# Four token tiles together in the first FFN, and modulation sums queued behind row scaling

## The chip, the cores and the metric

The kernel runs on one core of one Trainium2 chip. The metric is the device time of one execution in microseconds (us). A core has five engines that work side by side, each through its own list of instructions in order: TensorE (PE, matrix products; its weight loads are listed as PEld), VectorE (DVE), ScalarE (ACT), GpSimd (POOL) and SyncE (SP, which here only issues transfers, DMAs, from the chip's memory). Matrix products write to PSUM, and VectorE and ScalarE read from there.

## The reference

The network has two layers over 256 latent tokens and 256 context tokens of 1024 channels, in fp32. Cut to what matters here, it computes:

```python
def modulate(h, g_pre, shift, scale):
    return rms_norm(h, g_pre) * (1 + scale) + shift

def modulation(cond, w, b):            # nine rows of 1024 per condition
    m = jax.nn.silu(cond) @ w + b
    ...

def half_ffn_update(h, mod, k, g_pre, g_post, w_in, w_out):
    y = swiglu(modulate(h, g_pre, mod[3 * k], mod[3 * k + 1]), w_in, w_out)
    return h + FFN_RES_WEIGHT * mod[3 * k + 2] * rms_norm(y, g_post)

for i in range(DEPTH):
    mx = modulation(c, w_mod[i], b_mod[i])
    mc = modulation(c_ctx[None], w_mod[i], b_mod[i])
    x = half_ffn_update(x, mx, 0, ...)        # and the same for the context with mc
    ...                                       # layer 0: recurrent mixer, layer 1: attention
    x = half_ffn_update(x, mx, 2, ...)
```

`swiglu` multiplies by `w_in` (1024 x 5632, a gate half and an up half), forms silu(gate) * up, and multiplies by `w_out` (2816 x 1024).

## The kernel before

**Tiles and precision.** The 512 tokens are four tiles of 128: 0 and 1 are context (`CTX`), 2 and 3 latent (`LAT`), worked in the order 2, 3, 0, 1 (`TILES`). Each fp32 operand is split in two fp32r parts: ScalarE casts the high part (`whi`, `hh`, `dh`, line 114), VectorE subtracts it from the source for the low part (`wlo`, `hl`, `dl`, line 115). A product is three matmuls: high by high, high by low, low by high (lines 151 to 153 in `punit`). A weight tile is loaded by `wslot` into one of five slots (`raw`), 512 KB each; the same five slots take the modulation rows of the background jobs.

**FFN.** `ffn` goes through 22 column blocks of 128 hidden units. For one block `punit` runs a gate unit and an up unit (u = 0, 1) over eight channel blocks k, and `glu` (lines 408 to 414) forms the product and splits it. In a normal FFN the first four columns (`NSPLIT`) run for the latent tokens and then for the context tokens, 256 wide, because the context tiles come later out of the stage before; all other columns run for all 512 tokens. After each group of columns `w_out` is applied.

**The opening.** The very first FFN has no stage before it. `ffn_start` takes its place for the first four columns: in two channel halves (hb) it computes the shift and scale rows by matmuls (`mods_start`, line 295), turns them to columns, applies them to the turned latent rows (`first_pre`, lines 271 to 273), and runs the four columns for the latent tokens. Then `load_ctx` loads, scales and turns the context tiles, and `ffn` runs the four columns for them. `first_scale` and `first_turn` scale the rows and turn them by TensorE (line 201).

**Between stages.** When a stage has the result of a tile, `post` scales it and adds it to the residual stream, and `pre` computes the next row scaling: a mean of squares on ScalarE (line 172), eight VectorE instructions on one value per row (`rstd`, lines 181 to 188), and the scaling (line 194). `pre_turn` follows some units later, turns the tile on TensorE (line 201) and applies shift and scale on ScalarE (line 239).

**Background jobs.** The other modulation rows are computed by VectorE. `mod_job` loads eight pieces of `w_mod` and adds each, times a value of the condition, to a sum (line 365, 1024 wide), for one or both conditions; then a TensorE matmul with ones adds over partitions (line 371), a ScalarE copy (line 392) takes the row out of PSUM and TensorE turns it into columns (line 280), or the row is multiplied by a gain and spilled (lines 378 to 388). `bg(n)` runs n steps of the jobs at marked points of an FFN.

**Order of the work.** No order is written out by hand. The program lists the instructions; when the kernel is built a planner goes through them with a model of their costs, takes among those whose inputs it thinks are there the one listed first (those under `high_priority` ahead), and so fixes one order for each engine and the DMA queue. On the chip each engine follows that order and waits where an input is late. `order(ins)` gives what is listed under it an edge: it comes behind `ins` on that engine.

Of the kernel before, what the change touches and what calls it, by code (L numbers as in the profile page):

```python
# [11 lines left out]
ALU = mybir.AluOpType  # L12
# [24 lines left out]
class Net:  # L37
    def __init__(self, ctx, tc):
# [4 lines left out]
        self.pending = []  # L43
        e = ctx.enter_context
# [209 lines left out]
    def first_scale(self, t):  # L254
        return self.scaled(t, self.m4().rearrange("p a b -> p (a b)"))
# [8 lines left out]
    def first_pre(self, cond, A, S, ks=range(NK)):  # L264
        nc = self.nc
        s = (CTX, LAT)[cond]
# [57 lines left out]
    def ffn_start(self, w_in, w_mod, between):  # L324
        v = w_in.rearrange("(k p) c -> p k c", p=P)
        self.A00 = self.c([P, NK, 2], F32, "A00")
        banks = [self.mm().rearrange("p (u t) -> p u t", u=2) for _ in range(NSPLIT)]
        ws = [[] for _ in range(NSPLIT)]
        for hb in range(2):
            first = self.mods_start(w_mod, hb, between)  # L330
            self.first_pre(1, *first, range(4 * hb, 4 * hb + 4))
            for p in range(NSPLIT // 2):
                for u in range(2):
                    ws[2 * p + u].append(
                        self.wslot([v[:, 4 * hb : 4 * hb + 4, u * DFF + p * 256 : u * DFF + p * 256 + 256]])
                    )
                for o in range(2):
                    for u in range(2):
                        w = [ws[2 * p + u][hb]] * 2
                        self.punit(  # L340
                            banks[2 * p + o][:, u],
                            w,
                            o,
                            LAT,
                            range(4 * hb, 4 * hb + 4),
                            hb == 0 and u == 0,
                            hb == 1,
                        )
                    if hb == 1:
                        self.glu(banks[2 * p + o][:, 0], banks[2 * p + o][:, 1], 2 * p + o, LAT)  # L350
        return ws, first

    def mod_job(self, l, m, conds=(0, 1), f=None):
# [7 lines left out]
        for k in range(NK):  # L361
            raw = self.raw()
            nc.sync.dma_start(raw, self.w_mod[l, k * P : (k + 1) * P, m * D : (m + 1) * D])
            for c in conds:
                v.scalar_tensor_tensor(acc[c], raw, self.cs[:, k, c : c + 1], acc[c], op0=ALU.mult, op1=ALU.add)  # L365
            yield
        ps = self.st()
# [10 lines left out]
        if f is not None:  # L378
            gq = self.s2()
            gi = 3 + m // 3  # L380
            for j in range(4):
                cc = slice((j // 2) * 512, (j // 2) * 512 + 512)
                nc.gpsimd.dma_start(gq[32 * j : 32 * j + 32], self.norm_g[l, gi : gi + 1, cc].to_broadcast((32, 512)))
            row = self.a2()
# [713 lines left out]
```

## Time and profile before

| What | us |
|---|---|
| median of three runs | 1713.89 |
| the three runs | 1711.07, 1713.89, 1714.55 |
| the profiled execution, its own time | 1710.77 |
| its span in the trace | 1709.0 |

The page gives busy times of each engine, the chain of work that ended last, and the costliest groups of instructions. A line of the timeline reads: start, duration, engine, line of the kernel, operation, output tile from input tiles, shapes, how many were merged, and in brackets how long the engine stood idle before it and what ended that. Matmuls overlap, so the distance between two starts tells their rate and not the duration. A line of the windows reads: stretch, its length, busy time of PE, PEld, DVE, ACT and POOL with counts, the granted clock of TensorE as a share of 2.4 GHz, the busy share of the DMA engines, and GB/s.

### The profile page before, as it was taken

The numbers are of one execution on the slowest core, as the hardware profiler recorded it, in microseconds if no ns is written. First come the engines' busy times: TensorE is split into PE (matmuls) and PEld (weight loads), VectorE is DVE, ScalarE is ACT, GpSimd is POOL, SyncE is SP. The second block draws the span as 40 slices with busy tenths as digits, with TensorE's granted clock in tenths as the row PEclk, the third lists the DMA queues.
The fourth block names the chain that finished last, engine by engine and source line by source line (L and its number), as shares of the span: only waits on it lengthen the run. The fifth ranks groups of instructions, "written<-read, shape, count | busy, mean of one in ns | idle before, by whom it ended". The sixth has DMA issues, their size and how long they took to land.

```text
span 1709.0 us, 22391 instructions
## 1 busy us (share of the span) xinstructions
PE 1658.0 (97%) x8744; PEld 1385.9 (81%) x8744; DVE 1118.7 (65%) x1705; ACT 704.7 (41%) x1117; POOL 44.2 (3%) x89
## 2 busy tenths in 40 slices
PE   6999999999999989999999999999999999999997
PEld 4978888888988788888888888878888886679997
DVE  4878677658978785877833695655433687575454
ACT  3423322236699442332222442332232466574442
POOL 0010000000000001000000001000000000000000
PEclk9999999999999999999999999999999999999999
DMA  9366655443233154666433055865332061046561
GB/s 341 132 207 214 202 174 177 147 162 99 79 95 99 50 198 133 211 205 198 156 116 98 26 197 164 293 197 172 108 109 96 29 218 50 1 152 210 169 202 45
DMA packets 163961, 253.39 MB, mean 148 GB/s; under 512 B 9600, under 2 KB 114664, under 8 KB 163856
## 3 DMA queue, kind: packets, MB, share of 16 engines
q1 hardware_dynamic: 159424, 244.35, 43.8%
q0 software_dynamic: 3680, 7.10, 1.4%
q8 instruction: 68, 1.11, 0.3%
q10 hardware_dynamic: 752, 0.53, 0.1%
q14 instruction: 37, 0.30, 0.1%
HBM read 250.84 MB, written 1.10 MB: 147 GB/s over the span
## 4 chain that ended last, share of the span: by engine, by line
PE 77%; DVE 10%; ACT 5%; DMA 5%; issue 2%; ACTq 0%; DVEq 0%
PE mm L151 15%; PE mm L153 15%; PE mm L152 15%; PE mm L166 7%; PE mm L168 7%; PE mm L167 7%; DVE m L365 3%; DMA raw<-in_w_mod_dram 2%; DVE wlo L115 2%; PE mm L877 1%; DMA raw<-in_ffn_w_out_dram 1%; DMA raw<-in_ffn_w_in_dram 1%; ACT whi L114 1%; PE st L914 1%; PE st L903 1%
## 5 line engine op out<-in xcount | busy, mean ns | idle before, releaser
L151 PE MATMUL mm<-hh,whi 128*128 128x512 f32 (+1 forms) x1808 | 615.8, 342 | 8.3 <-ACT hh L271 4.7
L152 PE MATMUL mm<-hl,whi 128*128 128x512 f32 (+1 forms) x1808 | 615.7, 341 | 1.4 <-DVE hl L115 1.0
L153 PE MATMUL mm<-hh,wlo 128*128 128x512 f32 (+1 forms) x1808 | 616.3, 341 | 0.3 <-DVE wlo L115 0.3
L115 DVE TENSOR_TENSOR wlo<-raw,whi 128x1024 fp32r<-128x1024 f32 x316 | 382.4, 1221 | 157.0 <-ACT whi L114 155.3
L114 ACT CAST whi<-raw 128x1024 fp32r<-128x1024 f32 x316 | 330.2, 1053 | 353.4 <-DMA raw<-in_ffn_w_in_dram 107.5
L151 PEld LDWEIGHTS mm<-hh,whi 128*128 128x128 f32 x1808 | 346.0, 192 | 54.4 <-ACT hh L271 5.4
L152 PEld LDWEIGHTS mm<-hl,whi 128*128 128x128 f32 x1808 | 346.5, 192 | 39.5 <-DVE hl L115 1.4
L153 PEld LDWEIGHTS mm<-hh,wlo 128*128 128x128 f32 x1808 | 346.8, 192 | 38.1 <-DVE wlo L115 0.6
L365 DVE SCALAR_TENSOR_TENSOR m<-raw,cs,m 128x1024 f32<-128x1024 f32 x224 | 277.0, 1278 | 47.1 <-DMA raw<-in_w_mod_dram 39.2
L166 PE MATMUL mm<-whi,dh 128*128 128x512 f32 x592 | 232.7, 393 | 4.7 <-ACT dh L114 2.4
L168 PE MATMUL mm<-whi,dl 128*128 128x512 f32 x592 | 231.2, 391 | 0.0
L167 PE MATMUL mm<-wlo,dh 128*128 128x512 f32 x592 | 231.0, 390 | 0.0
L413 DVE TENSOR_TENSOR a<-s,mm 128x512 f32<-128x512 f32 (+1 forms) x96 | 54.5, 568 | 171.0 <-PE mm L153 111.8
L166 PEld LDWEIGHTS mm<-whi,dh 128*128 128x128 f32 x592 | 111.6, 188 | 34.0 <-issue 3.4
L412 ACT ACTIVATE s<-mm 128x512 f32<-128x512 f32 (+1 forms) x96 | 48.3, 503 | 214.1 <-PE mm L153 214.1
L168 PEld LDWEIGHTS mm<-whi,dl 128*128 128x128 f32 x592 | 111.6, 188 | 23.9 <-DVE dl L115 0.4
L167 PEld LDWEIGHTS mm<-wlo,dh 128*128 128x128 f32 x592 | 111.5, 188 | 22.4
L114 ACT CAST dh<-a 128x512 fp32r<-128x512 f32 (+1 forms) x96 | 50.5, 526 | 187.6 <-DVE a L413 187.6
L115 DVE TENSOR_TENSOR dl<-a,dh 128x512 fp32r<-128x512 f32 (+1 forms) x96 | 54.6, 569 | 26.5 <-ACT dh L114 26.3
L239 ACT ACTIVATE tmp<-st,modT,A 128x128 f32<-128x128 f32 x144 | 54.6, 468 | 9.3 <-PE st L201 9.3
L482 DVE TENSOR_TENSOR y<-y,mm 128x512 f32<-128x512 f32 x24 | 16.5, 686 | 38.1 <-PE mm L168 38.1
L172 ACT ACTIVATE tmp<-y 128x1024 f32<-128x1024 f32 x12 | 12.7, 1058 | 58.5 <-DVE y L434 58.5
(212 smaller groups left out, 1311.6 us busy)
## 6 DMA issues: line engine op xcount, KB each, us to landing
raw<-in_ffn_w_in_dram SPq DMA_DIRECT2D x176, 512.0 KB, 4.8
raw<-in_w_mod_dram SPq DMA_DIRECT2D x128, 512.0 KB, 4.4
raw<-in_ffn_w_out_dram SPq DMA_DIRECT2D x88, 512.0 KB, 4.8
wm<-in_w_mod_dram SPq DMA_DIRECT2D x16, 512.0 KB, 7.2
raw<-in_rg_w_in_dram SPq DMA_DIRECT2D x16, 512.0 KB, 3.3
raw<-in_attn_w_qkv_dram SPq DMA_DIRECT2D x12, 512.0 KB, 3.7
g<-spill POOLq DMA_DIRECT2D x16, 256.0 KB, 4.4
raw<-in_rg_gate_w_dram SPq DMA_DIRECT2D x16, 256.0 KB, 3.2
```

What stands on the lines that cost most here:

```text
L114: self.nc.scalar.copy(hi, src)
L115: self.nc.vector.tensor_tensor(lo, src, hi.bitcast(F32), op=ALU.subtract)
L151: nc.tensor.matmul(out, a, xh, start=first and k == ks[0], stop=False, skip_group_check=True)
L152: nc.tensor.matmul(out, a, xl, start=False, stop=False, skip_group_check=True)
L153: nc.tensor.matmul(out, b, xh, start=False, stop=last and k == ks[-1], skip_group_check=True)
L166: nc.tensor.matmul(out, a, wh, start=(k == 0), stop=False)
L167: nc.tensor.matmul(out, a, wl, start=False, stop=False)
L168: nc.tensor.matmul(out, b, wh, start=False, stop=(k == nk - 1))
L239: nc.scalar.activation(hf[:, k * P : (k + 1) * P], ps[:, q * P : (q + 1) * P], AF.Identity, bias=S[:, k, cond : cond + 1], scale=A[:, k, c ...
L365: v.scalar_tensor_tensor(acc[c], raw, self.cs[:, k, c : c + 1], acc[c], op0=ALU.mult, op1=ALU.add)
L412: nc.scalar.activation(a, pg, AF.Silu)
L413: nc.vector.tensor_tensor(b, a, pu, op=ALU.mult)
```

## The change

Three things are changed. First, in the opening all four token tiles are loaded, scaled and turned before the first modulation half is applied; only the first two columns run there, for all 512 tokens and in two channel halves; columns 2 and 3 join the ordinary ones. The turned tiles are copied out of PSUM by ScalarE instead of VectorE. Second, the sums of the background jobs get an edge to the last row scaling that `pre` listed (`chain`), and the end of each job (`mod_sum`, `mod_cols`) is listed at the next background step instead of right behind the sums. Third, a small silu activation is listed at the end of the recurrent mixer.

```diff
     def scaled(self, t, xs):
-        self.nc.vector.tensor_scalar(xs, self.x[:, t], r, RS, op0=ALU.mult, op1=ALU.mult)
+        self.last = self.nc.vector.tensor_scalar(xs, self.x[:, t], r, RS, op0=ALU.mult, op1=ALU.mult)
...
     def pre(self, t, A, S, buf):
         with self.tc.high_priority():
             xs = self.scaled(t, buf)
+        self.chain = self.last
...
     def first_turn(self, t, xs):
         for b in range(2):
             ps = self.turn(xs, b)
-            self.nc.vector.tensor_copy(
+            self.nc.scalar.copy(
...
         for k in ks:
-            a, b = A[:, k, cond : cond + 1], S[:, k, cond : cond + 1]
-            tmp = self.tmp()[:, :HT]
-            nc.scalar.activation(self.hh[:, k, s], yt[:, k, s], AF.Identity, bias=b, scale=a)
-            nc.vector.tensor_scalar(tmp, yt[:, k, s], a, b, op0=ALU.mult, op1=ALU.add)
-            nc.vector.tensor_tensor(self.hl[:, k, s], tmp, self.hh[:, k, s].bitcast(F32), op=ALU.subtract)
+            tmp = self.tmp()[:, :T]
+            for cond, s in ((1, LAT), (0, CTX)):
+                a, b = A[:, k, cond : cond + 1], S[:, k, cond : cond + 1]
+                nc.scalar.activation(self.hh[:, k, s], yt[:, k, s], AF.Identity, bias=b, scale=a)
+                nc.vector.tensor_scalar(tmp[:, s], yt[:, k, s], a, b, op0=ALU.mult, op1=ALU.add)
+            nc.vector.tensor_tensor(self.hl[:, k], tmp, self.hh[:, k].bitcast(F32), op=ALU.subtract)
...
     def ffn_start(self, w_in, w_mod, between):
+        banks = [[self.mm() for u in range(2)] for o in range(2)]
         for hb in range(2):
+            ks = range(4 * hb, 4 * hb + 4)
             first = self.mods_start(w_mod, hb, between)
+            self.first_pre(*first, ks)
+            ws = [[self.wslot([v[:, 4 * hb : 4 * hb + 4, u * DFF : u * DFF + 256]])] * 2 for u in range(2)]
+            for o in range(2):
                 for u in range(2):
+                    self.punit(banks[o][u], ws[u], o, ALL, ks, hb == 0, hb == 1)
+        for o in range(2):
+            self.glu(*banks[o], o, ALL)
...
             for c in conds:
-                v.scalar_tensor_tensor(acc[c], raw, self.cs[:, k, c : c + 1], acc[c], op0=ALU.mult, op1=ALU.add)
+                with self.order(self.chain):
+                    v.scalar_tensor_tensor(acc[c], raw, self.cs[:, k, c : c + 1], acc[c], op0=ALU.mult, op1=ALU.add)
+            if k == NK - 1:
+                self.later.append(lambda: self.mod_sum(l, m, acc, f))
             yield
...
+    def finish_later(self):
+        todo, self.later = self.later, []
+        for f in todo:
+            f()
...
     def load_ctx():
-        between = [norm_cols] + [lambda t=t: N.first_turn(t, xs[t]) for t in TILES[:2]]
-        ws, first = N.ffn_start(ffn_w_in[0, 0], w_mod, between)
-        for t in TILES[2:]:
-            nc.sync.dma_start(N.x[:, t], cx[0, t * P : (t + 1) * P, :])
-            N.first_turn(t, N.first_scale(t))
-        N.first_pre(0, *first)
+        between = [lambda t=t: N.first_turn(t, xs[t]) for t in TILES]
+        between[0] = lambda: (norm_cols(), N.first_turn(TILES[0], xs[TILES[0]]))
+        N.ffn_start(ffn_w_in[0, 0], w_mod, between)
         rg_cols()
...
         def step(n):
+            N.finish_later()
             while n > 0:
...
+    with N.order(prev):
+        sc.activation(N.small([P, 1]), c1[:, 0:1], AF.Silu)
```

`mod_sum` holds the matmul with ones and either the gain and spill or the copy on ScalarE; it lists `mod_cols`, the turn into columns, for the step after. At the end of an FFN whatever is left of both is listed before the rows are loaded.

## Rows read from the trace of the kernel before

**Rows 1.** The page's first part: busy time, share of the span and number of instructions of each engine.

```profile
PE 1658.0 (97%) x8744; PEld 1385.9 (81%) x8744; DVE 1118.7 (65%) x1705; ACT 704.7 (41%) x1117; POOL 44.2 (3%) x89
```

**Rows 2.** Busy times in four stretches: the opening, the first four columns of the second FFN, those of the third, and a place in the third FFN.

```profile
0.00:84.70 84.70, 68.50 (x492) 58.11 (x493) 55.12 (x139) 32.21 (x54) 4.36 (x12) 0.94 0.68 238
602.20:659.70 57.50, 51.18 (x401) 50.33 (x400) 44.11 (x69) 25.00 (x49) 0.00 (x0) 0.94 0.51 168
985.20:1040.40 55.20, 50.95 (x401) 49.91 (x400) 45.72 (x71) 24.49 (x48) 0.00 (x0) 0.94 0.56 184
...
1143.20:1149.20 6.00, 3.41 (x12) 2.76 (x12) 4.43 (x7) 1.10 (x2) 0.03 (x1) 0.72 0.89 301
```

**Rows 3.** The waits of PE over the whole span: what waited for what, total us, times, longest.

```profile
PE st L201 <- DVE y L194: 5.7, 4, 2.5
```

**Rows 4.** The timeline of PE at the start of the second FFN.

```profile
608.08 0.28 PE L152 MATMUL mm<-hl,whi 128*128 128x256 f32 x1
608.20 0.28 PE L153 MATMUL mm<-hh,wlo 128*128 128x256 f32 x1
610.09 1.09 PE L201 MATMUL st<-ident,y 128*128 128x128 f32 x8 [1.62 <-DVE small L183]
...
629.77 1.09 PE L201 MATMUL st<-ident,y 128*128 128x128 f32 x8 [1.68 <-DVE y L194]
632.88 0.74 PE L151 MATMUL mm<-hh,whi 128*128 128x256 f32 x4 [2.02 <-ACT hh L114]
...
640.33 0.29 PE L151 MATMUL mm<-hh,whi 128*128 128x256 f32 x1
```

**Rows 5.** The timeline of DVE: two lines of the first FFN, then the scalings of tiles 0 and 1 at the second FFN and of tile 1 at the third.

```profile
59.67 0.72 DVE L272 TENSOR_SCALAR tmp<-y,A,modT 128x256 f32<-128x256 f32 x2
...
98.87 0.69 DVE L115 TENSOR_TENSOR dl<-a,dh 128x512 fp32r<-128x512 f32 x1
...
608.02 1.28 DVE L365 SCALAR_TENSOR_TENSOR m<-raw,cs,m 128x1024 f32<-128x1024 f32 x1
...
609.29 0.75 DVE L194 TENSOR_SCALAR y<-xres,small 128x1024 f32<-128x1024 f32 x1
...
621.25 0.15 DVE L181 TENSOR_SCALAR small<-small 128x1 f32<-128x1 f32 x1
...
628.97 0.74 DVE L194 TENSOR_SCALAR y<-xres,small 128x1024 f32<-128x1024 f32 x1
...
1011.36 0.73 DVE L194 TENSOR_SCALAR y<-xres,small 128x1024 f32<-128x1024 f32 x1
```

**Rows 6.** Busy time of line 365 alone in two stretches; the columns are the stretch, its length, DVE's busy time with the count, granted clock, DMA share and GB/s.

```profile
607.90:629.00 21.10, 14.00 (x11) 1.00 0.50 171
993.50:1011.40 17.90, 11.40 (x9) 1.00 0.45 152
```

**Rows 7.** The timeline of PE in the third FFN: the turn of a modulation row.

```profile
1145.93 1.11 PE L280 MATMUL st<-ident,s 128*128 128x128 f32 x4 [2.59 <-ACT s L392]
```

**Rows 8.** The timeline of DVE in the third FFN: sums that wait for their rows.

```profile
1109.06 1.29 DVE L365 SCALAR_TENSOR_TENSOR m<-raw,cs,m 128x1024 f32<-128x1024 f32 x1 [6.20 <-DMA raw<-in_w_mod_dram]
1113.80 1.29 DVE L365 SCALAR_TENSOR_TENSOR m<-raw,cs,m 128x1024 f32<-128x1024 f32 x1 [1.48 <-DMA raw<-in_w_mod_dram]
...
1139.38 1.28 DVE L365 SCALAR_TENSOR_TENSOR m<-raw,cs,m 128x1024 f32<-128x1024 f32 x1 [1.54 <-DMA raw<-in_w_mod_dram]
```

**Rows 9.** The timeline of PE in the opening.

```profile
17.22 1.93 PE L295 MATMUL st<-wm,cs 128*32 128x512 f32 x16
...
21.88 0.50 PE L151 MATMUL mm<-hh,whi 128*128 128x256 f32 x2 [1.35 <-ACT hh L271]
...
37.46 3.64 PE L295 MATMUL st<-wm,cs 128*32 128x512 f32 x32
...
43.81 0.74 PE L151 MATMUL mm<-hh,whi 128*128 128x256 f32 x4 [1.35 <-ACT hh L271]
...
59.84 1.05 PE L151 MATMUL mm<-hh,whi 128*128 128x256 f32 x4 [2.01 <-ACT hh L271]
...
84.72 0.40 PE L151 MATMUL mm<-hh,whi 128*128 128x512 f32 x1
84.95 0.40 PE L152 MATMUL mm<-hl,whi 128*128 128x512 f32 x1
```

**Rows 10.** The DMA issues of the first 60 us: the loads of the context rows, their number, size and median us to landing.

```profile
xres<-in_ctx_dram SPq DMA_DIRECT2D x2, 512.0 KB, 9.6
```

**Rows 11.** Busy times in two microseconds of the opening; the last column is GB/s.

```profile
12.00:14.00 2.00, 2.00 (x12) 1.65 (x16) 1.18 (x6) 0.00 (x0) 0.00 (x0) 1.00 1.04 385
```

**Rows 12.** The timeline of ScalarE: the copy of the first modulation row, and the start of the second FFN.

```profile
19.24 0.59 ACT L305 COPY s<-st 128x512 f32<-128x512 f32 x1 [8.94 <-PE st L295]
...
607.96 1.28 ACT L412 ACT_TABLE_LOAD   x1
609.26 0.39 ACT L412 ACTIVATE s<-mm 128x256 f32<-128x256 f32 x1
```

More of the change, by code (lines that the diff above doesn't have):

```diff
@@ L43, in __init__ @@
         self.pending = []
+        self.later = []
+        self.chain = None
         e = ctx.enter_context
@@ L254, in first_scale @@
     def first_scale(self, t):
-        return self.scaled(t, self.m4().rearrange("p a b -> p (a b)"))
+        return self.scaled(t, (self.m4() if t >= 2 else self.g4()).rearrange("p a b -> p (a b)"))
     def first_turn(self, t, xs):
@@ L364, in mod_job, with mod_sum @@
             for c in conds:
-                v.scalar_tensor_tensor(acc[c], raw, self.cs[:, k, c : c + 1], acc[c], op0=ALU.mult, op1=ALU.add)
+                with self.order(self.chain):
+                    v.scalar_tensor_tensor(acc[c], raw, self.cs[:, k, c : c + 1], acc[c], op0=ALU.mult, op1=ALU.add)
+            if k == NK - 1:
+                self.later.append(lambda: self.mod_sum(l, m, acc, f))
             yield
+    def mod_sum(self, l, m, acc, f):
+        nc = self.nc
+        v = nc.vector
         ps = self.st()
@@ L377, in mod_job, with mod_cols @@
                 )
[L378 to L384, printed above, removed]
-            v.scalar_tensor_tensor(row, ps, f * RS, gq, op0=ALU.mult, op1=ALU.mult)
-            spill = self.tc.dram_tile([4, 512], F32, name=self.nm("spill"))
-            nc.gpsimd.dma_start(spill, row[0:P:32])
-            self.rows[l, m] = spill
-            yield
-            return
-        row = self.s2()
-        nc.scalar.copy(row, ps)
-        yield
+        if f is None:
+            row = self.s2()
+            nc.scalar.copy(row, ps)
+            self.later.append(lambda: self.mod_cols(l, m, row))
+            return
+        gq = self.s2()
+        gi = 3 + m // 3
+        for j in range(4):
+            cc = slice((j // 2) * 512, (j // 2) * 512 + 512)
+            nc.gpsimd.dma_start(gq[32 * j : 32 * j + 32], self.norm_g[l, gi : gi + 1, cc].to_broadcast((32, 512)))
+        row = self.a2()
+        v.scalar_tensor_tensor(row, ps, f * RS, gq, op0=ALU.mult, op1=ALU.mult)
+        spill = self.tc.dram_tile([4, 512], F32, name=self.nm("spill"))
+        nc.gpsimd.dma_start(spill, row[0:P:32])
+        self.rows[l, m] = spill
+    def mod_cols(self, l, m, row):
         tv = self.cols_of(row)
         for hb in range(2):
-            v.tensor_copy(self.modT[:, l, m, hb * 4 : hb * 4 + 4, :], tv[:, :, 64 * hb : 64 * hb + 64 : 32])
-        yield
+            self.nc.vector.tensor_copy(
+                self.modT[:, l, m, hb * 4 : hb * 4 + 4, :], tv[:, :, 64 * hb : 64 * hb + 64 : 32]
+            )
+    def finish_later(self):
+        todo, self.later = self.later, []
+        for f in todo:
+            f()
     def pre_cols(self, l, k, conds=(0, 1)):
@@ L441, in ffn @@
         vo = w_out.rearrange("(j p) c -> p j c", p=P)
-        if mid is None:
-            ws = [w for p in range(NSPLIT // 2) for w in self.ffn_w(w_in, p)]
-        else:
-            ws = mid()
-        for s in (LAT, CTX):
-            if s is LAT and mid is not None:
-                continue
-            for j in range(NSPLIT):
-                ps = self.mm().rearrange("p (u t) -> p u t", u=2)
-                for u in range(2):
-                    self.punit(ps[:, u], ws[2 * (j // 2) + u], j % 2, s)
-                    self.tick(1)
-                self.glu(ps[:, 0], ps[:, 1], j, s)
-                if mid is None or s is CTX:
+        n0 = 2
+        if mid is not None:
+            mid()
+        else:
+            n0 = NSPLIT
+            ws = [w for p in range(NSPLIT // 2) for w in self.ffn_w(w_in, p)]
+            for s in (LAT, CTX):
+                for j in range(NSPLIT):
+                    ps = self.mm().rearrange("p (u t) -> p u t", u=2)
+                    for u in range(2):
+                        self.punit(ps[:, u], ws[2 * (j // 2) + u], j % 2, s)
+                        self.tick(1)
+                    self.glu(ps[:, 0], ps[:, 1], j, s)
                     bg(1)
@@ L458, in ffn @@
             for j in range(j0, j1):
-                if j < NSPLIT:
+                if j < n0:
                     continue
@@ L469, in ffn @@
                 bg(1000)
+                while self.later:
+                    self.finish_later()
                 rows()
@@ L519, in net_kernel @@
     N.w_mod, N.b_mod, N.norm_g = w_mod, b_mod, norm_g
-    for t in TILES[:2]:
-        nc.sync.dma_start(N.x[:, t], x[0, (t - 2) * P : (t - 1) * P, :])
+    for t in TILES:
+        nc.sync.dma_start(N.x[:, t], x[0, (t - 2) * P : (t - 1) * P, :] if t >= 2 else cx[0, t * P : (t + 1) * P, :])
     N.ident = N.c([P, P], F32, "ident")
@@ L538, in net_kernel @@
     nc.scalar.dma_start(cr[8:16], c.rearrange("b (k p) -> (b k) p", p=P))
-    xs = {t: N.first_scale(t) for t in TILES[:2]}
+    xs = {t: N.first_scale(t) for t in TILES}
     sc.activation(csr, cr, AF.Silu)
```

26 lines of the change are left out of this document (1 added, 25 removed).

## The prediction

> **What bounds the kernel now.** I read the page first: the matrix engine is busy 97% of the span [rows 1], so an edit can gain only where this engine waits or runs at its lower clock. Next I cut the span into windows of 1 us, looked for those with little PE work or a granted clock under 1, and took the stretches around them as single windows [rows 2]. In such a row the reader compares PE's busy time with the length, and then reads the clock column. Three places stand out that the diff touches: the opening up to column 4 of the first FFN (84.7 us long, PE busy 68.5), the start of the second FFN (57.5 us, clock 0.94), and the start of the third (55.2 us, clock 0.94); a small fourth one is at 1143. The waits of PE say what ended them: turns of scaled rows wait for the row scaling L194 four times, 5.7 us in all [rows 3].
>
> The timeline of PE at the second FFN shows two stops: it issues until 608.2 and again at 610.1, stops for tile 1 until 629.8, then again until 632.9, and only at 640.3 do its matmuls take 0.29 us again, at 2.4 GHz after a spell at 1.2 [rows 4]. The timeline of DVE tells why [rows 5]: tile 0's scaling at 609.3 stands behind a modulation sum (L365) of 1.28 us, and tile 1's chain of eight tiny instructions, from 621.25 to the scaling at 628.97, has a sum between nearly every two. In 607.9 to 629.0 DVE is never idle and 14.0 us of it are eleven sums; at the third FFN nine sums take 11.4 of 17.9 us, and tile 1's scaling comes at 1011.4 [rows 5, 6].
>
> **The change part by part.**
>
> *Sums behind the row scaling.* Each L365 gets an edge to the last scaling of the boundary before it, so the 11 and 9 sums leave these stretches. How much that frees: two halves of four columns are 384 matmuls of 256, issued 0.12 us apart (608.08, 608.20 [rows 4]), 46.1 us; two turns are 1.1 us each by the row at 610.09. The window to column 4 is 57.5 us [rows 2], so 57.5 - 46.1 - 2.2 = 9.2 us are lost at the second FFN, half-clock time included, and 55.2 - 48.3 = 6.9 us at the third. Without 14.0 us of sums tile 1's scaling, 628.97 today, could end at 615; its path also runs through ScalarE and a residual addition, so I take 619. PE is inside the latent columns until about 628, so the planner can place the turn among them. Left over I put 1 us each, for a turn that the planner places a little too early (tile 0's stop was 1.8 us, of which the 1.28 us sum goes). Gain: 8.2 + 5.9 = 14.1 us; the bounds are 0 (the planner leaves the turn where it was) and 16.1.
>
> *What queues behind the new wait.* DVE runs in order; the planner knows the edge, so weight subtractions go ahead of a waiting sum. What waits is the sum's own raw tile: five such slots serve modulation rows and weights together. From 619 on DVE has eight rows, sixteen sums, at 1.27 us (14.0/11 [rows 6]) 20 us, plus the weight subtractions of column 4, which PE wants at 659.7 - 8.2 = 651. 619 + 20 + 5 = 644: hidden by 7 us, and less at the third FFN. If the rows landed late, DVE would idle as at 1109 and 1113.8, where single sums stand 4.7 us apart for want of a load [rows 8]. I charge 3 us for both places, between 0 and the 25 us of the slow rival below, nearer to 0 because by the planned order the loads have ten free us.
>
> *Sum and columns split off (mod_sum, mod_cols), run at the next background step.* The same matmuls and transposes are issued, later. At 1145.9 PE stands 2.6 us for the ScalarE copy L392 between the two [rows 7], because DVE had waited for a modulation row (1139.4, [rows 8]) and ScalarE behind it. One step later the copy is long done. The window is 6 us with PE busy 3.4 and clock 0.72 [rows 2]: 2.6 us idle, and half clock over 2 x 0.28 x 6 = 3.4 us costs up to 1.7. I take 3.5 us; the bounds are 0 (another late row finds another victim) and 4.3. The sum's GpSimd issues (four gain rows and a spill) go a step later with it; the rows are read only at the stage's end. Jobs now need 8 steps instead of 9 or 10, so they end earlier within a stage; nothing waits for that.
>
> *The opening.* Before: the last matmuls of the first modulation half start at 17.2, the first FFN matmul at 21.9, those of the second half run 37.5 to 41.1, the next matmul is at 43.8, the context half starts at 59.8 and column 4 at 84.7 [rows 9]. After: two context loads of 512 KB, 0.52 MB, stand ahead of the modulation weights on SP's queue [rows 10]; at 385 GB/s [rows 11] that is 2.7 us. First matmul: 21.9 + 2.7, and 0.4, about half of a 1.1 us turn, for the fourth tile's = 25.0. The first half has 48 matmuls of 512, 0.23 us apart (84.72, 84.95), 10.9 us against 11.5 for the 96 of before; these took 15.6 (21.9 to 37.5), so 4.1 are half clock and waits, which stay: 25.0 + 15.0 = 40.0. The second half's modulation matmuls and the chain from them to the FFN's take 43.8 - 37.5 = 6.3: 46.3. In the second half the first unit follows DVE: per channel block two affine steps, 0.72, and one subtraction of 512, 0.69 [rows 5], 1.4 us against 0.7 of PE; four blocks 5.6, then 36 matmuls, 8.3: 60.2. Columns 2 and 3, 96 matmuls: 22.1, so column 4 starts at 82.3 against 84.7, 2.4 us sooner. What goes is the wait for the context rows at 59.8 with its half clock; what is late next is the modulation chain. Two FFN weight tiles instead of four stand ahead of the second modulation half in program order, so its weights land no later than today, and the planner may run its matmuls inside the first half; then up to 6.3 more goes. Against it, half clock may come back at 46 to 52 (2.5 us) and the four scalings may be late. I take 2, bounds -3 and +8. The turned copies move from DVE to ScalarE, which stood idle for 8.9 us before 19.2 [rows 12]; no cost.
>
> *Table load at the end of the recurrent mixer.* It is 1.28 us at 607.96, and the next activation starts 0.02 us after its end [rows 12]. It moves into a stretch of ScalarE without haste. It hides at present behind PE's stop at 608 to 610; with that stop gone it would have delayed the next turn's evictions, so moving it keeps my 8.2 whole: 0 of its own, bounds 0 and 1.3. The Trainium skill, "ScalarE: Activation LUTs", section "What ACT_TABLE_LOAD costs", adds a drain of about 1380 ns to the load, some 2.7 us a switch; the row here shows the 1283 ns alone. By the page the sum would be 1.4 us better at most, and only if the load stood on PE's path.
>
> **Sum.** 14.1 - 3 + 3.5 + 2 = 16.6 us off. The profiled execution took 1710.8 us (span 1709.0), so one like it would take 1694.2. The median of the runs shown is 3.1 above that execution; I shift by 0.8 and say 1695.
>
> **Rivals.**
> - *Given back.* The delayed sums come back as late weights at columns 4 and 5 of both FFNs, or as a new wait of a kind with the one at 1145.9. For it: DVE is full in both stretches [rows 6], and a row of sums now arrives in a burst. Against it: behind 640 DVE has room (it is busy 65% of the span [rows 1]). Half of 14.1 stays, the rest as above: 7 - 3 + 3.5 + 2 = 9.5, about 1701 to 1706.
> - *The opening overlaps.* The planner runs the second modulation sums inside the first half: 6 us more, about 1688. For it: fewer FFN weights stand ahead of them. Against it: the first half keeps PE ready work of higher rank.
> - *Slower: the rows starve behind the edge.* Five raw slots are held by rows that wait for tile 1's scaling; the next rows and column 4's weights are loaded only as slots come free. If eight rows came 4.7 us apart, as at 1109 [rows 8], the burst would last 38 us from 619, to 657, and the first weights would follow at some 660: 9 us behind 651, with 3 us of half clock, twice. That is -24 against +14.1, the late chain at 1145 stays, the opening gives 2: 8 us slower, 1719. It decides from 31/8 = 3.9 us a row on (619 to 650). Against it: with the slots full and all rows landed, five of eight cost only 2.5 us each.
> - *It doesn't do what it says.* The planner leaves the turns where they are; then the 3.5 and 2 remain: 1705 to 1709.
>
> **How the numbers follow.** Forecast 0.56 (1689 to 1700), given back 0.16, no effect at the boundaries 0.10, opening overlaps 0.09, starved rows 0.09. The range, 1685 to 1710, leaves the slow case and a little of the fast end out. This kernel's runs lie 3.5 us apart, 0.2%, and closer than that nothing is told from no change. Faster by over 0.2% means under 1710.5: 0.86; within 0.2%: 0.06, from the weak cases' upper ends; slower 0.08.
>
> **What would show it.** In the profile of after: no L365 between 600 and the last L194 of either boundary; PE without a stop over 1 us and clock 1.0 in the two windows, each near 49 us instead of 57.5 and 55.2; no wait of L280 for L392; column 4 of the first FFN near 82 us, with the wait at 59.8 gone. I am wrong if PE waits for weights after column 3, if a turn still waits for L194 by over 2 us, or if column 4 starts after 87 us.

## The result, and the profile after

The changed kernel takes 1697.78 us (median of five runs, 1696.84 to 1700.36), the kernel before 1712.01 beside it: ratio 0.9921, 95% interval 0.9904 to 0.9937. The profiled execution took 1696.84 with a span of 1695.0, 14.0 below the span of before. So 14 us are to be found, and the forecast of 16.6 was nearly met. Term by term it was met for the wrong reasons in two places.

The page still has PE at 97% [rows 1]; its busy time fell by 7.1 us, from 1658.0, so about half of the 14 us were time in which PE stood and half time in which it counted as busy:

```profile
PE 1650.9 (97%) x8552; PEld 1367.1 (81%) x8552; DVE 1112.6 (66%) x1681; ACT 707.7 (42%) x1118; POOL 44.2 (3%) x89
```

Windows of the places of [rows 2], and one more (672.8 to 712.1, the first products with w_out of the second FFN); the columns are busy us of PE, PEld, DVE, ACT and POOL with counts, then granted clock, DMA share and GB/s:

```profile
0.00:85.50 85.50, 66.34 (x300) 45.45 (x301) 60.04 (x124) 38.47 (x58) 4.37 (x12) 0.94 0.79 271
600.30:649.80 49.50, 48.13 (x401) 47.81 (x400) 42.75 (x67) 21.85 (x47) 0.00 (x0) 1.00 0.58 194
980.60:1030.00 49.40, 48.26 (x401) 47.82 (x400) 44.03 (x69) 22.28 (x46) 0.00 (x0) 1.00 0.61 202
672.80:712.10 39.30, 37.74 (x158) 28.57 (x157) 33.67 (x32) 11.54 (x15) 1.00 (x2) 0.96 0.64 207
```

The second and third row are the gain: the two FFN starts last 49.5 and 49.4 us where they lasted 57.5 and 55.2, at full clock. The first row is no gain: the opening up to column 4 is 85.5 us long, and was 84.7. The fourth row is a loss: these 156 matmuls (144 with w_out, and 12 of the background jobs among them) took 34.4 us before.

The waits of PE (us in all, times, longest): the turn waits for the row scaling 4.0 instead of 5.7 [rows 3], the wait of the modulation turn for its copy [rows 7] is gone, and a wait for the cast dh of 1.6 us is new.

```profile
PE st L546 <- ACT tmp L544: 8.4, 1, 8.4
PE mm L153 <- ACT hh L274: 5.1, 2, 2.6
PE st L203 <- DVE y L196: 4.0, 4, 1.4
PE mm L168 <- ACT dh L116: 2.6, 2, 1.6
```

On DVE's timeline at the second FFN the edge is seen at work: tile 1's scaling ends its chain at 615.21, where [rows 5] has 628.97, and the first sum (now L355) stands right behind it. PE's turn of tile 0 waits once, 1.37 us.

```profile
614.77 0.16 DVE L190 SCALAR_TENSOR_TENSOR small<-small,small 128x1 f32<-128x1 f32 x1
614.87 0.42 DVE L416 TENSOR_TENSOR a<-s,mm 128x256 f32<-128x256 f32 x1
615.21 0.75 DVE L196 TENSOR_SCALAR y<-xres,small 128x1024 f32<-128x1024 f32 x1
615.87 1.28 DVE L355 SCALAR_TENSOR_TENSOR m<-raw,cs,m 128x1024 f32<-128x1024 f32 x1
```

For the accounting I read six stretches from PE's timeline, each between the starts of two matmuls, in the kernel before, in the changed one, and later in every experiment (us, one execution each; the last column is the run's ratio to the kernel before, timed beside it):

- A: start of the span to the first product with w_out; less 21.8 it is the start of column 4
- B: from there to column 6, behind the first group of w_out (it holds a stop near 110 us)
- C, E: first matmul to column 4 of the second and third FFN
- D: second FFN, first product with w_out to column 6
- F: third FFN, column 6 to the second group of w_out (the stop near 1143)

| kernel | A | B | C | D | E | F | ratio |
|---|---|---|---|---|---|---|---|
| before | 106.5 | 36.9 | 57.6 | 34.4 | 55.2 | 92.9 | |
| changed | 107.3 | 35.5 | 49.5 | 39.2 | 49.4 | 90.3 | 0.9921 |
| changed, again | 106.7 | 35.2 | 49.5 | 37.2 | 49.2 | 90.3 | 0.9913 |
| edge alone | 107.7 | 36.4 | 49.7 | 34.4 | 49.6 | 95.5 | 0.9912 |
| deferral alone | 106.4 | 35.1 | 57.4 | 34.4 | 56.3 | 90.4 | 0.9972 |
| opening alone | 106.5 | 33.9 | 57.8 | 34.4 | 55.4 | 95.4 | 0.9988 |
| changed, old opening | 108.7 | 35.4 | 49.8 | 36.9 | 49.8 | 90.3 | 0.9907 |
| only columns deferred | 108.0 | 33.9 | 49.6 | 34.4 | 49.2 | 89.8 | 0.9870 |
| the same, again | 107.3 | 33.9 | 49.6 | 34.4 | 49.1 | 89.9 | 0.9852 |
| the same, old opening | 107.0 | 35.7 | 49.8 | 34.4 | 49.3 | 89.9 | 0.9892 |
| early modulation | 101.2 | 38.3 | 49.9 | 39.7 | 49.2 | 90.4 | 0.9887 |
| early and columns | 101.1 | 33.9 | 49.3 | 34.4 | 49.0 | 89.9 | 0.9830 |
| w_out ahead | 107.7 | 36.6 | 51.5 | 34.4 | 49.9 | 90.3 | 0.9880 |
| early and columns, no early Silu | 101.2 | 33.9 | 49.8 | 34.4 | 49.1 | 89.9 | 0.9827 |

Before to changed: A +0.8, B -1.4, C -8.0, D +4.9, E -5.8, F -2.6, together -12.1 of the 14.0. Of the rest, 1.4 is a spell at half clock near 559 us, in a stretch that the change doesn't touch: the window 555 to 570 has clock 0.89 in the kernel before and 1.00 in the changed one with the same 12.75 us of PE work, and in the second execution of the changed kernel it is 0.89 again. That part was luck of the profiled execution.

Two things needed an explanation: the loss in D, and the opening that gained nothing.

### The profile page after: what moved, and what is told of

The parts are those of the page before. It is cut to its first block, busy times and chain, and to the rows that moved or that the text cites. A ratio compares the mean times of both kernels' runs of the same rounds, so it can differ in the third digit from the quotient of the medians.

```text
span 1695.0 us, 21965 instructions
## 1 busy us (share of the span) xinstructions
PE 1650.9 (97%) x8552; PEld 1367.1 (81%) x8552; DVE 1112.6 (66%) x1681; ACT 707.7 (42%) x1118; POOL 44.2 (3%) x89
## 4 chain that ended last, share of the span: by engine, by line
PE 50%; DVE 5%; DMA 2%; ACT 2%; issue 1%; DVEq 0%; POOL 0%; ACTq 0%; POOLq 0%
PE mm L155 9%; PE mm L153 9%; PE mm L154 9%; PE mm L168 5%; PE mm L170 5%; PE mm L169 5%; DMA raw<-in_ffn_w_in_dram 1%; PE mm L880 1%; DVE wlo L117 1%; PE st L917 1%; PE st L906 1%; PE st L976 1%; PE st L977 1%; PE st L978 1%; DVE m L355 1%
## 5 line engine op out<-in xcount | busy, mean ns | idle before, releaser
L153 PE MATMUL mm<-hh,whi 128*128 128x512 f32 (+1 forms) x1744 | 603.7, 347 | 5.1 <-ACT hh L274 5.1
L154 PE MATMUL mm<-hl,whi 128*128 128x512 f32 (+1 forms) x1744 | 602.2, 346 | 1.4 <-DVE hl L276 1.4
L155 PE MATMUL mm<-hh,wlo 128*128 128x512 f32 (+1 forms) x1744 | 602.0, 345 | 0.2 <-DVE wlo L117 0.2
L153 PEld LDWEIGHTS mm<-hh,whi 128*128 128x128 f32 x1744 | 331.2, 190 | 54.0 <-issue 7.5
L154 PEld LDWEIGHTS mm<-hl,whi 128*128 128x128 f32 x1744 | 331.4, 190 | 42.2 <-DVE hl L276 2.4
L155 PEld LDWEIGHTS mm<-hh,wlo 128*128 128x128 f32 x1744 | 331.1, 190 | 40.4 <-DVE wlo L117 0.6
L355 DVE SCALAR_TENSOR_TENSOR m<-raw,cs,m 128x1024 f32<-128x1024 f32 x224 | 277.0, 1278 | 20.3 <-DMA raw<-in_w_mod_dram 18.2
L416 DVE TENSOR_TENSOR a<-s,mm 128x512 f32<-128x512 f32 (+1 forms) x92 | 53.9, 586 | 149.7 <-PE mm L155 100.6
L116 ACT CAST dh<-a 128x512 fp32r<-128x512 f32 (+1 forms) x92 | 49.7, 540 | 162.1 <-DVE a L416 162.1
```

The source lines that it names most:

```text
L116: self.nc.scalar.copy(hi, src)
L153: nc.tensor.matmul(out, a, xh, start=first and k == ks[0], stop=False, skip_group_check=True)
L154: nc.tensor.matmul(out, a, xl, start=False, stop=False, skip_group_check=True)
L155: nc.tensor.matmul(out, b, xh, start=False, stop=last and k == ks[-1], skip_group_check=True)
L416: nc.vector.tensor_tensor(b, a, pu, op=ALU.mult)
```

## The experiments

### The parts alone

The edge alone (the kernel before, with these lines):

```
+ self.last = self.nc.vector.tensor_scalar(xs, self.x[:, t], r, RS, ...)
+ self.chain = self.last
+ with self.order(self.chain):
      v.scalar_tensor_tensor(acc[c], raw, self.cs[:, k, c : c + 1], acc[c], ...)
```

> The kernel before with the edge alone: every modulation sum is ordered behind the last row scaling; sums and columns still follow at the old steps, and the opening is the old one. Theory (the edge carries the change, and the new stop of PE near 677 us of the changed kernel comes from the deferred sums, which free their accumulators late): column 4 of the second FFN comes 8 us sooner after that FFN's first matmul than before (49.5 us instead of 57.6), of the third 6 us sooner (49.4 instead of 55.2), and no wait of PE for the ScalarE cast dh of over 1 us stands near 677: ratio 0.9925, some 1699 us. Rival (the edge itself gives its gain partly back, the burst of sums holds DVE in front of the gated product): the two stages are as short, but the stop of 1.5 us with its half clock stands there as well and costs 5 us behind column 4: ratio 0.9950, some 1703 us. In both the stop of 2.6 us near 1143 is still there.

Measured 1699.69 against 1714.77 us: 0.9912, 0.9898 to 0.9927. C and E are as short as in the changed kernel and D has no stop. The theory holds: all of the edge's 13.4 us arrive and nothing is given back in D. The stop of the third FFN is still there, here with a wait of 5.22 us (F is as long with the opening alone); the row is PE's timeline:

```profile
1133.51 1.11 PE L283 MATMUL st<-ident,s 128*128 128x128 f32 x4 [5.22 <-ACT s L396]
```

The deferral alone (the kernel before, with mod_sum, mod_cols and finish_later):

```
+ if k == NK - 1:
+     self.later.append(lambda: self.mod_sum(l, m, acc, f))
  yield
...
+ N.finish_later()
```

> The kernel before with the deferral alone: the sum over partitions and the turned columns of a modulation row are issued one background step later; no edge, old opening. Theory: the two FFN starts stay at 57 and 55 us, the stop near 1143 (PE waits for the ScalarE copy of the sums) goes with its half clock, 3.5 us: ratio 0.9980, some 1708.5 us; accumulators that come free late may cost up to 3 of it behind column 4 of the second FFN. Rival (the stop at 1143 went because the edge moved all sums, or because the jobs end sooner): the stop is still there, ratio 1.000.

Measured 1709.27: 0.9972, 0.9960 to 0.9984. F falls by 2.6 us, and the stretch from column 6 of the third FFN to its third group of w_out by 4.1. The stop went by the deferral, as forecast. Of the rest of its gain 1.8 us lie in B and 1.5 in the spell near 559, which was absent here; E is 1.0 us longer.

The opening alone (first_scale, first_pre, ffn_start, load_ctx and the four loads ahead):

```
- for t in TILES[:2]:
-     nc.sync.dma_start(N.x[:, t], x[0, ...])
+ for t in TILES:
+     nc.sync.dma_start(N.x[:, t], x[0, ...] if t >= 2 else cx[0, ...])
```

> The kernel before with the new opening alone: four tiles scaled and turned at once, two columns for all tokens in two channel halves; no edge, no deferral. Theory (two more row loads of 512 KB ahead of the modulation weights delay the first FFN matmul by 6.7 us, and the second half's weights still wait for a slot as before): the first product with w_out starts at 107.3 instead of 106.5, ratio 1.0000 to 1.0010. Rival (the opening gains its 2 us as forecast and something else in the changed kernel ate it before 107 us): the product starts at 104.5, ratio 0.9988.

Measured 1712.06: 0.9988, 0.9978 to 0.9999. The ratio is the rival's, the place is neither's. Column 4 came when it came before (A is the same 106.5), yet the run is about 2 us faster: B is 33.9, the stop near 110 is gone. The gain lies behind the opening.

The changed kernel with the old opening:

> The changed kernel with the old opening (edge, deferral and the moved table load kept). Theory: the opening is worth nothing or costs 1 us, so this is as fast as the changed kernel or 1 us faster: ratio 0.9910 to 0.9922, 1696.5 to 1698.5 us. Rival (the opening earns 2 us, and the later stages give them back): ratio 0.9932, 1700 us.

Measured 1698.87: 0.9907, 0.9892 to 0.9921, so the old opening looks no slower; in the later pair (columns alone deferred, 0.9870 with the new opening and 0.9892 with the old) the new one looks faster. The intervals overlap in both pairs, and these timings say no more than that the opening is worth between nothing and 4 us. But the three parts alone multiply to 0.9912 x 0.9972 x 0.9988 = 0.9872, 22 us, and the changed kernel has 14. Together the parts lose 7 to 8 us. Where, D shows: 34.4 with any part alone, 37 to 39 with edge and deferral together.

### Why the parts don't add up

At the loss, PE waits for the cast dh, and the cast for the gated product (L416). PE's timeline has the wait:

```profile
677.94 0.50 PE L168 MATMUL mm<-whi,dh 128*128 128x512 f32 x1 [1.56 <-ACT dh L116]
```

DVE's timeline shows what stands ahead of it:

```profile
664.29 1.23 DVE L117 TENSOR_TENSOR wlo<-raw,whi 128x1024 fp32r<-128x1024 f32 x1 [5.03 <-ACT whi L116]
665.44 0.68 DVE L416 TENSOR_TENSOR a<-s,mm 128x512 f32<-128x512 f32 x1
666.03 0.68 DVE L385 SCALAR_TENSOR_TENSOR a<-st,s 128x512 f32<-128x512 f32 x1
666.88 0.91 DVE L348 MEMSET m<- 128x1024 f32 x1 [0.17 <-issue]
667.71 0.63 DVE L117 TENSOR_TENSOR dl<-a,dh 128x512 fp32r<-128x512 f32 x1
668.50 0.91 DVE L348 MEMSET m<- 128x1024 f32 x1 [0.16 <-issue]
670.18 2.60 DVE L355 SCALAR_TENSOR_TENSOR m<-raw,cs,m 128x1024 f32<-128x1024 f32 x2 [0.77 <-DVE m L348]
672.96 3.68 DVE L355 SCALAR_TENSOR_TENSOR m<-raw,cs,m 128x1024 f32<-128x1024 f32 x3 [0.18 <-DMA m<-in_b_mod_dram]
676.56 0.68 DVE L416 TENSOR_TENSOR a<-s,mm 128x512 f32<-128x512 f32 x1
```

DVE idles 5 us for the third weight of w_out, then everything follows late: the older product, the memsets, five sums of the next job, and only then the product, whose cast PE wants at 676.4 (677.94, where it goes on, less its wait of 1.56). The weight is late because its load found no raw slot. SP's queue in the changed kernel (start, time from the first issue to the last, count):

```profile
638.78 5.25 SPq L352 DMA_DIRECT2D raw<-in_w_mod_dram  x4
644.83 14.82 SPq L125 DMA_DIRECT2D raw<-in_ffn_w_out_dram  x3
```

Four rows of the next job stand before the three weights, and there are five raw slots. In the edge alone three rows stand there, and the last of the three weights is issued by 653.4 instead of 659.7:

```profile
640.17 3.30 SPq L366 DMA_DIRECT2D raw<-in_w_mod_dram  x3
644.28 9.16 SPq L125 DMA_DIRECT2D raw<-in_ffn_w_out_dram  x3
```

What put the fourth row there is the deferral, in a way that I had noted and thought harmless ("they end earlier within a stage; nothing waits for that"): once the sum is no step of its own, the next job's rows start a step earlier in program order. If so, it is enough to give the sum its step back and defer the columns alone:

```
- if k == NK - 1:
-     self.later.append(lambda: self.mod_sum(l, m, acc, f))
  yield
+ self.mod_sum(l, m, acc, f)
+ yield
```

> The changed kernel, but the sum over partitions is issued at its old step and only the turned columns follow one step later. Theory (the deferred sum moved the next job's rows one background step ahead, so four of its rows instead of three stand before the weights of w_out and hold the five raw slots; the third weight lands late, its subtraction holds DVE, and behind it the memset, the sums and the gated product): the product's w_out group of the second FFN runs without a stop, 34.4 us from its first product with w_out to the next column instead of 39.2, and the stop near 1143 stays gone since the turn still has a step between itself and the copy: ratio 0.9885 to 0.9895, 3 to 5 us under the changed kernel. Rival (the edge's burst and the deferral of the columns make the stop together): it stays, ratio as the changed kernel's within 0.001. Second rival: the stop near 1143 comes back (4 to 5 us) and takes what the other gives.

Measured 1690.97 against 1715.20: 0.9870, 0.9846 to 0.9894; timed a second time:

> The run with only the columns deferred, unaltered, beside the next two on another occasion. Theory (the parts add up once the jobs start at their old steps: 0.9912 x 0.9972 x 0.9988 = 0.9872): ratio 0.986 to 0.989 again. Rival (0.9870 was a lucky run): 0.990 or more.

1690.41 against 1716.54: 0.9852, 0.9838 to 0.9867. The changed kernel itself stood beside the first of these:

> The changed kernel itself, unaltered, beside the next three on one chip. Both theories: ratio 0.991 to 0.992, column 4 of the first FFN between 84.5 and 86 us, the stop of PE near 677 us with its half clock, about 5 us between column 4's end and column 8 of the second FFN more than the 34.4 us of the kernel before.

1698.73: 0.9913, 0.9894 to 0.9933 (the 5 us that its expectation places behind column 4 are D's, 2.9 in this execution). So one step of a background job costs this change 7 to 8 us by the times, more than the 3 to 5 expected, and with it the parts add up. In the two traces of the changed kernel D and B hold 6.5 and 4.2 of it; the rest is not located. SP's queue has three rows there again, and DVE idles 0.27 us ahead of its sums; the product (L416) stands at 671.42, 3 us before PE can want its cast (D begins at 671.15, and in the changed kernel PE came to it 3.6 us into D):

```profile
637.10 2.97 SPq L352 DMA_DIRECT2D raw<-in_w_mod_dram  x3
641.30 8.30 SPq L125 DMA_DIRECT2D raw<-in_ffn_w_out_dram  x3
```

```profile
662.71 0.91 DVE L348 MEMSET m<- 128x1024 f32 x1 [0.16 <-issue]
663.89 7.39 DVE L355 SCALAR_TENSOR_TENSOR m<-raw,cs,m 128x1024 f32<-128x1024 f32 x6 [0.27 <-DVE m L348]
671.42 0.69 DVE L416 TENSOR_TENSOR a<-s,mm 128x512 f32<-128x512 f32 x1
```

D is 34.4 with full clock. Not all of its loss was the stop: the changed kernel issues the eight matmuls with ones of a background job in two batches, at 693.15 and 698.21, where this one and the kernel before issue them together, and the second batch costs about 1.2 us in either trace. The stop and the half clock behind it are the other 3.7 us (1.6 in the second execution). F is as short as in any kernel, so the second rival (the stop near 1143 comes back) is out as well. B fell too, to 33.9: the same pattern stands in the first FFN, where the changed kernel issues four rows and then three weights at 90.12 in 14.63 us, and this one three rows and the weights in 7.18.

This leaves two accounts of the loss: the raw slot, or the accumulators, which a later sum frees later. They part if the weights go ahead of the rows while sum and columns both stay deferred:

```
+ if j == j1 - 2 and gi < len(GROUPS) - 1:
+     ws0 = self.wrows(vo, j0, j1, 0)
  bg(2)
...
- ws = self.wrows(vo, j0, j1, cb)
+ ws = self.wrows(vo, j0, j1, cb) if cb else ws0
```

> The changed kernel with the first three weights of w_out loaded one background step earlier, ahead of the next job's rows; sum and columns both deferred as in the changed kernel. Theory (the stop near 677 comes from the third weight, which waits for a raw slot behind four rows): no stop of over 0.5 us at the first product with w_out of either the first or the second FFN, 34.4 us from there to the next column in the second; ratio 0.987 to 0.989, unless the eight rows that now stand before the second three weights stop PE there instead, 11 us on. Rival (the accumulators that the deferred sum frees late make it): the stop at 677 stays at 1 to 1.6 us with its half clock, ratio 0.991 to 0.992.

Measured 1697.08 against 1716.54: 0.9880, 0.9861 to 0.9899. D is 34.4: the stop near 677 went with the weights' place alone, and the sums are as late in program order as in the changed kernel. The slot is the cause there; the eight matmuls with ones stand together again as well. In the first FFN it only moved: eight rows now stand before the second three weights, and PE stops there for dh, 1.56 us at 112.83. So B is 36.6. C is longer by 2 us: PE waits 1.82 us at 611.52 for the row scaling of tile 0, which comes at 610.71 on DVE (606.04 in the changed kernel) with six weight subtractions between the steps of its chain, and from 611.9 to 615.3 the clock is at 1.2 GHz. The kernel is 5 us slower by the ratios, 7 by the medians, than the one with the columns alone deferred, timed on the same occasion. First SP's queue, then the stop:

```profile
73.96 18.28 SPq L352 DMA_DIRECT2D raw<-in_w_mod_dram  x8
94.31 13.47 SPq L125 DMA_DIRECT2D raw<-in_ffn_w_out_dram  x3
```

```profile
112.83 0.51 PE L168 MATMUL mm<-whi,dh 128*128 128x512 f32 x1 [1.56 <-ACT dh L116]
```

The old opening with the columns alone deferred:

> As the run with the columns alone deferred, but with the old opening. Theory (the new opening is worth 0 to 1 us): ratio within 0.0007 of that run's. Rival (the new opening earns the 2 us forecast): 0.0012 above it or more.

Measured 1695.45: 0.9892, 0.9876 to 0.9908, by its middle 3.8 us behind the new opening beside it, with overlapping intervals. Its B is 35.7 against 33.9: 1.8 of that are the stop near 110, on the side of the rival, though not by the way it names, since A is 107.0 against 108.0.

### Why column 4 came no sooner

In the changed kernel the first half begins late. PE's timeline:

```profile
22.46 1.09 PE L203 MATMUL st<-ident,g 128*128 128x128 f32 x8
23.48 1.06 PE L298 MATMUL st<-wm,cs 128*32 128x512 f32 x8
25.25 0.66 PE L283 MATMUL st<-ident,s 128*128 128x128 f32 x4 [0.71 <-ACT s L308]
28.55 0.79 PE L153 MATMUL mm<-hh,whi 128*128 128x512 f32 x1 [2.64 <-ACT hh L274]
```

The modulation matmuls end at 24.5 instead of 19.2, since their loads are issued from 4.84 on instead of 1.66 and the turns of four tiles stand between them. The chain from there to the first FFN matmul takes 4.0 us instead of 2.7, since PE now needs the latent and the context half of a channel block before it can start on all 512 tokens: it starts behind the third activation (27.9 to 28.5), where it started behind the first before (wait 2.64 against 1.35 [rows 9]). Between the halves it is the same chain again, as long as it could be:

```profile
43.11 3.64 PE L298 MATMUL st<-wm,cs 128*32 128x512 f32 x32
47.45 0.66 PE L283 MATMUL st<-ident,s 128*128 128x128 f32 x4 [0.71 <-ACT s L308]
50.57 1.28 PE L153 MATMUL mm<-hh,whi 128*128 128x512 f32 x4 [2.46 <-ACT hh L274]
```

These matmuls waited for nothing at 43.11, but their weights came just in time: the last of the eight loads landed 12.5 us after its issue, at 45.6, and the four matmuls that use it start at 46.1. SP's queue has six FFN weights ahead of these loads, as before; the sixth waits for a slot and goes out by 29.3, and only then the eight modulation loads follow, while the DMA engines move 0 to 9 GB/s from 27 to 30 us. SP's queue, then the last of the eight loads:

```profile
11.00 18.32 SPq L125 DMA_DIRECT2D raw<-in_ffn_w_in_dram  x6
29.37 4.65 SPq L295 DMA_DIRECT2D wm<-in_w_mod_dram  x8
```

```profile
L295 SPq DMA_DIRECT2D wm<-in_w_mod_dram x1: 934/934/934, 33.1 to 33.1; - x1
DMA to landing us min/median/max: 12.5/12.5/12.5
```

So both the queue and PE's order keep the second modulation half behind the first FFN half, and with the queue as it is another order of PE alone could have gained about 0.6 us by these rows (an estimate). The experiment moves both:

```
- w = self.ffn_w(w_in, j // 2)
+ with self.order(self.wm_last):
+     w = self.ffn_w(w_in, j // 2)
...
+ if hb == 0 and o == 1:
+     first = self.mods_start(w_mod, 1, between)
+     last = self.mod_last
+ with self.order(last):
      self.punit(banks[o][u], ws[u], o, ALL, ks, hb == 0, hb == 1)
```

> The changed kernel with the second half's modulation ahead: its eight weight loads go before those of columns 2 and 3 on SP's queue, and its matmuls go between the first and the second column of the first channel half. Theory (the opening gained nothing because the second half's chain of 7.5 us, 43.1 to 50.6, of which 3.6 us are its matmuls, followed the first half instead of running inside it): no gap between the two channel halves but the matmuls themselves; column 4 of the first FFN starts at 81 to 82 us instead of 85.5, ratio 0.9895, 3 to 4 us under the changed kernel. Rival (the loads are what sets the time, the DMA engines cannot bring the second half's weights before 40 us): PE waits for them inside the first half and column 4 starts at 85 or later, no gain.

Measured 1695.42 against 1715.20: 0.9887, 0.9872 to 0.9902. Column 4 starts at 79.4, 6 us sooner, and there is no wait between the halves: the matmuls run at 37.00 to 40.6 inside the first half, and their turn at 41.61 waits for nothing.

```profile
37.00 3.64 PE L299 MATMUL st<-wm,cs 128*32 128x512 f32 x32
41.61 0.60 PE L284 MATMUL st<-ident,s 128*128 128x128 f32 x4
```

The order was the cause, not the transfer: the same eight loads, issued from 17.7 on, were there in time. Only 3 (by the medians) to 4 of the 6 us reach the end, because PE arrives earlier at the loads of w_out, with four rows before the third weight as in the changed kernel: B is 38.3. With the columns alone deferred this should go:

> Both mended: only the columns deferred, and the second half's modulation ahead of columns 2 and 3. Theory (the loads of three rows, not four, stand before the third weight of w_out in the first and second FFN): column 4 of the first FFN near 79.5 us, no stop of PE at its products with w_out (4 us lost at 104 to 112 in the run with early modulation alone), none at the second's; 5 to 6.5 us under the run with the columns alone: ratio 0.983 to 0.984. Rival (the first FFN's rows are late whatever the order, now that PE comes 6 us sooner): the stop at 104 to 112 stays, 2 us gained: 0.986.

Measured 1687.47 against 1716.54: 0.9830, 0.9811 to 0.9848, as the theory says; A is 101.1, B 33.9, D 34.4. Against the columns alone deferred, timed beside it, that is 3 to 4 us, less than the 5 to 6.5 expected, and the intervals overlap; the 6.2 us in A are plain in the trace. This version is 29 us faster than the kernel before, and by the medians 10, by the ratios 14 us faster than the changed one; its opening shows what was open there, 64.5 us of PE work in 79.3 at clock 0.98 where [rows 2] has 68.5 in 84.7:

```profile
0.00:79.30 79.30, 64.47 (x300) 44.40 (x301) 58.43 (x122) 37.59 (x57) 4.35 (x12) 0.98 0.85 287
```

### The table load

The last term of the forecast, taken out of this fastest version:

```
- with N.order(prev):
-     sc.activation(N.small([P, 1]), c1[:, 0:1], AF.Silu)
```

> The kernel with both parts mended, without the early Silu at the end of the recurrent mixer, so that the table load falls at the second FFN's first gated product again. Theory (my step: the load is worth nothing of its own on PE's path): the second FFN's stage to column 4 stays at 49.3 to 49.8 us; ratio 0.983 within 0.001. Rival (with PE's stop gone the load delays the evictions behind the next turn): that stage is 50.6 us or longer.

Measured 1684.99 against 1715.30: 0.9827, 0.9810 to 0.9845; C is 49.8 against 49.3, and 0.3 of that is the turn of tile 0, which waits 1.50 us for its scaling, ahead of the load. ScalarE's rows:

```profile
602.08 1.18 ACT L243 ACTIVATE tmp<-st,modT,A 128x128 f32<-128x128 f32 x3
603.28 1.28 ACT L421 ACT_TABLE_LOAD   x1
604.58 0.39 ACT L421 ACTIVATE s<-mm 128x256 f32<-128x256 f32 x1
```

The load falls behind the turn's evictions and is worth nothing, as forecast. It takes 1.28 us, begins 0.02 us after the activation before it and ends 0.02 us ahead of the next. The Trainium skill, "ScalarE: Activation LUTs", section "What ACT_TABLE_LOAD costs", adds a drain of about 1380 ns; no row here shows one.

## Why the prediction was right or wrong

- **Bound.** Right: PE sets the time, and what was gained was gained where it stopped or ran at half clock.
- **Sums behind the row scaling, 14.1 us.** Right in size and cause: C -8.0 and E -5.8 (8.2 and 5.9 forecast), and the edge alone gives 7.8 and 5.6. Tile 1's scaling came at 615.2, not 619; PE didn't need it that soon. The 1 us left at each place is the first turn's wait, 1.37 and 1.02.
- **Late sums, -3 us.** The cause was wrong, and that D's loss is near 3 us is luck. The burst of sums hid as worked out: the edge alone gives back nothing, and the weights of column 4 were ready. What was lost, 4.9 us in D in the profiled execution (2.9 in the second), came from deferral and edge together. The step that failed is "they end earlier within a stage; nothing waits for that": the third weight of w_out waits for a raw slot, 14.8 us from the first issue to the third instead of 8.3. I had traced the slots only for columns 4 and 5. Against the parts alone the interaction cost 7 to 8 us by the times, with the stop in B that it kept, so the term was too small by 4 to 5.
- **Deferral, 3.5 us.** Right: the wait of the turn for its copy is gone in every kernel with deferred columns, and F fell by 2.6, and by 3.1 with the columns alone deferred. The columns are what gains; the deferred sum did the harm.
- **Opening, 2 us by column 4 at 82.3.** Wrong: it started at 85.5, 0.8 later than before (84.9 in the second execution, 84.7 with the opening alone). The first step that failed is the first FFN matmul at 25.0: it came at 28.55, 2.3 of the difference from modulation matmuls spread between four tiles' turns and their later loads, 1.3 from a first channel block that is ready only behind the third activation. The chain between the halves, taken as 6.3, was 7.5 for the same reason. That the fewer weights ahead would let the second half overlap was wrong too: the planner put six there as before. What the opening did gain, it gained at the stop near 110 (B 33.9 alone), which no term held.
- **Table load and copies, 0.** Right for the table load. The copies on ScalarE were not tried by themselves.
- **Rivals.** "Given back" happened in part, not as late weights at columns 4 and 5 but one group later. "The opening overlaps", put at 6 us, did not happen by itself; made to, it brought 6 us at column 4. "Starved rows" did not happen at the boundaries. The total was right since the spell near 559 and the stop near 110 paid 2.8 us that no term held, part of what the opening and the larger loss were short.

## What to carry to other kernels

Deferring a step of a background job also pulls the rest of that job forward: count what its next loads do to the slots that they share with the loads on the path. Before crediting a stage with overlap, look whether the queue's order and the engine's order both allow it, since moving one instruction ahead is not enough when its loads still stand behind another's wait. And time the parts alone: where their product is better than the whole, the difference is an interaction that can be found.

## What the runs showed of the hardware

The length of a stop alone doesn't tell whether half clock follows it. In the changed kernel PE stopped for 1.56 us near 677, ran again at 2.4 GHz until about 679.6, and then at 1.2 GHz until 683.0; with the early modulation it stopped for 3.55 us at the same place and stayed at 2.4 GHz behind it. The rows are windows over the stop and behind it, first of the changed kernel, then of the other:

```profile
676.00:678.00 2.00, 0.44 (x3) 0.06 (x1) 2.00 (x3) 0.62 (x1) 0.00 (x0) 1.00 0.69 227
678.00:679.50 1.50, 1.50 (x6) 0.98 (x7) 1.50 (x3) 0.00 (x0) 0.00 (x0) 1.00 0.81 298
679.70:683.00 3.30, 3.30 (x9) 2.62 (x8) 3.30 (x4) 0.52 (x1) 0.00 (x0) 0.50 0.50 169
```

```profile
673.00:677.00 4.00, 0.45 (x3) 0.35 (x3) 4.00 (x4) 0.62 (x1) 0.00 (x0) 1.00 0.64 164
677.00:683.00 6.00, 6.00 (x27) 4.67 (x26) 6.00 (x7) 1.18 (x2) 0.00 (x0) 1.00 0.71 233
```

What decides it, the runs don't settle. The second execution of the changed kernel stopped for 1.1 us near 677 and lost no clock, so single executions of one kernel differ by 2 us here, and the opening by as much (A of the five kernels with the old opening: 106.4 to 108.7).
